# Weighted side steps, residual tiles one ahead, and inverse roots for four tiles at a time in a hybrid gMLP and state-space layer

## The chip, the cores and the metric

The kernel runs on one core of one Trainium2 chip. The metric is the device time of one execution, in microseconds (us). Engines are named as the profile names them: PE (TensorE, its weight loads as PEld), DVE (VectorE), ACT (ScalarE), POOL (GpSimd), and SP (SyncE), whose queue issues every DMA of this kernel in order.

## The reference

One layer over 2048 latent tokens of width 1024, in fp32. Cut to what matters here:

```
hl  = rms(x) * norm1_w * (1 + sc1) + sh1
proj = hl @ w_in                               # u, v (1024 each), z (1024), x/B/C (1536), dt
xbc = silu(conv5(x/B/C)); dt = softplus(dt + bias)
y   = scan_forward + scan_backward + xs * D    # 16 heads, 2 groups, state 128, chunks of 128 tokens
g   = (y * silu(z)) split in 2 groups of 512
ssd_out = rms(g over each group) * ssd_norm_w
u, v = gelu(u), gelu(v)
v   = rms(v over each head of 128) * gm_norm_w
gm_out = u * (W_s @ v + b_s)                   # 128x128 mixing per head and chunk
x   = x + g1 * (concat(gm_out, ssd_out) @ w_out)
x   = x + g2 * swiglu(rms(x) * norm2_w * (1 + sc2) + sh2)
out = rms(x) * final_norm_w
```

## The kernel before

Matrix products run as three fp32r products of high and low parts (`mm3`, lines 221 to 232): each weight tile and each activation tile is split into a rounded high part (ACT copy) and the remainder (DVE subtraction). One "product" below is a 128x512 output tile, 24 matmuls of 512 columns. The product tiles are in four PSUM banks (`mmp`), what the side work needs in four others (`smp`).

The tokens are worked in two blocks of 1024, block 1 first (projections v, u, z, then x/B/C), then block 0. After the x/B/C projection of block 0 comes the phase that the change is about. It has a main chain and a side chain, both Python generators that are interleaved when the program is written:

- Main chain: `proj_z(0)` (16 products), `proj_v(0)` (16), `proj_u(0)` (16), then three of the four parts of the output projection, `out_half(1,0)`, `out_half(0,0)` and `out_half(0,1)` (block, half; 16 products each). Half 0 takes the gMLP output, half 1 the scan output.
- Side chain: `ssd_bwd` (the backward states, 16 steps), then `ssd_y`, which goes over 16 chunks and 2 groups: `y_seg` (decay matrices: two DMAs of decay rows from `fscr`, 16 small operations on ACT and as many on DVE, an exponential, a POOL product), `y_out` (three products with py, pf and pb, sums, D term, product with z from `zscr`, sum of squares by ACT), `y_norm` (inverse root of both groups by `newton`, and two ACT copies with it as scale), `y_store` (four PE transposes per group, an ACT copy, a DMA to `sscr`).

`run` gives the main chain one step and the side chain 2.74 steps (SIDE) in turn, whatever the steps cost. The order of the generators sets the priorities of the instructions; each engine then executes its own queue in order, and the tile framework that emits the program may still move an instruction past others of its engine. `early` calls `load_mix` when the main chain has `lead` products left in a part, so that the next part's operands are loaded and split: 8 tiles for each half block, from `gmscr` or `sscr`, into `xin` buffers (8 exist) and then into `actt` buffers (16 exist, all taken by one part's operands).

`newton` (lines 234 to 244) computes an inverse root on a narrow tile by 11 small DVE operations. `proj_v` calls it once per product tile for 4 heads, `y_norm` once per chunk for 2 groups.

`out_half` computes, for each product, `t = product * g1 + t` with the residual tile t, which it loads into a buffer after the product's matmuls in program order (line 849), adds (line 850) and stores to `x2scr` (line 851). In half 1 it also sums squares, and `rstd_store` turns the sum into the inverse root for the next norm.

The last part, `out_half(1,1)`, runs beside `border()`, which prepares operands of the FFN (`prep_hl`, tiles kept for later in `cscr`). Then the buffers of the projections are given back, `hl_back` and `hl_split` (lines 978, 979, 1044) bring the FFN's operands, and `ffn1(0)` starts (matmuls at lines 1093 to 1095). In `ffn2` 16 residual tiles are held, the first NT2B in a pool of their own, the others in `t2` (14 buffers).

Of the kernel before, what the change touches and what calls it, by code (L numbers as in the profile page):

```python
# [14 lines left out]
P = 128  # L15
# [6 lines left out]
TB = 512  # L22
# [7 lines left out]
NT2B = 3  # L30
# [7 lines left out]
SIDE = 2.74  # L38
# [44 lines left out]
def kernel(ctx: ExitStack, tc: tile.TileContext, xT, ctxp, cc, crow, wad1, wad2, vecs, rows,  # L83
# [47 lines left out]
    rscr = [tc.dram_tile([1, TB], F32, name=f"rscr{i}") for i in range(4)]  # L131
    r2scr = [tc.dram_tile([1, TB], F32, name=f"r2scr{i}") for i in range(4)]
# [457 lines left out]
    def proj_u(blk, hs):  # L590
        for h0 in range(0, 8, 2):
            us = [unit(U_U + h0), unit(U_U + h0 + 1)]
            for j in range(2):
                ts_ = slice((blk * 2 + j) * TB, (blk * 2 + j + 1) * TB)
                for i, (hi, lo) in enumerate(us):
# [7 lines left out]
                    yield  # L603

    def proj_v(blk, hs):
# [17 lines left out]
        for hh in range(2):  # L623
            us = [unit(U_V + hh * 4 + i) for i in range(4)]
            for j in range(2):
                vh = []
                for c in range(4):
                    ps = mmp()
                    mm3(ps, stat_terms(hs, j * 4 + c, us, 0))
                    v = gelu2(ps, xin)  # L630
                    sq = tmp()
                    ms = sml()[:, :4]
                    for h in range(4):
                        S.activation(sq[:, h * P:(h + 1) * P], v[:, h * P:(h + 1) * P], AF.Square, accum_out=ms[:, h:h + 1])
                    V.tensor_scalar(out=ms, in0=ms, scalar1=1.0 / P, scalar2=4 * EPS, op0=ALU.mult, op1=ALU.add)
                    r = newton(ms, 4)
                    V.tensor_tensor(out=v[:, :TB].rearrange("p (a b) -> p a b", b=P), in0=v[:, :TB].rearrange("p (a b) -> p a b", b=P),
                                    in1=bc(r.rearrange("p (a o) -> p a o", o=1), P), op=ALU.mult)
                    vh.append(v)
                    if c == 1 and prev is not None:  # L640
                        mixing(*prev)
                    yield
                prev = (hh, j, vh)
        mixing(*prev)
        yield

    def proj_z(blk, hs):
        for g in range(2):
            us = [unit(U_Z + g * 4 + i) for i in range(4)]
            for c in range(8):  # L650
# [6 lines left out]
                yield  # L657
# [42 lines left out]
    def ssd_bwd(rp, hp, chunks):  # L700
        for c in chunks:
            for g in range(2):
# [4 lines left out]
                yield  # L707
# [7 lines left out]
    def y_seg(st, c, g):  # L715
        rc = st["rc"]
        Gt = []
        for q in range(2):
# [16 lines left out]
            yield  # L735
# [8 lines left out]
        yield  # L744

    def y_out(st, c, g, ms):
# [11 lines left out]
        yield  # L758
# [9 lines left out]
        yield  # L768
# [3 lines left out]
        S.activation(zt, ya, AF.Square, accum_out=ms[:, g:g + 1])  # L772
        yield
        return ya

    def y_norm(ys, ms):
        V.tensor_scalar(out=ms, in0=ms, scalar1=1.0 / TB, scalar2=4 * EPS, op0=ALU.mult, op1=ALU.add)
        r = newton(ms, 2)
        for g in range(2):
            S.activation(ys[g], ys[g], AF.Copy, scale=r[:, g:g + 1])  # L780
        yield

    def y_store(ys, c):
        for g in range(2):
            ps = smp()
            for i in range(4):
                PE.transpose(out=ps[:, i * P:(i + 1) * P], in_=ys[g][:, i * P:(i + 1) * P], identity=ident)
            t = tma()[:, :TB]
            S.copy(t, ps)
            DMA.dma_start(sscr[c // 4][g * TB:(g + 1) * TB, (c % 4) * P:(c % 4 + 1) * P].rearrange("(i p) t -> p i t", p=P),  # L790
                          t.rearrange("p (i t) -> p i t", t=P))
            yield

    def ssd_y(rp):
# [5 lines left out]
        ys, ms, norm, store = [], None, None, None  # L800
        for i, (c, g) in enumerate(its):
            if i + 1 < len(its):
                yield from y_seg(st[i + 1], *its[i + 1])
            if norm is not None:
                yield from y_norm(*norm[:2])
                norm, store = None, (norm[0], norm[2])
            if g == 0:
                ys, ms = [], sml()[:, :2]
            y = yield from y_out(st.pop(i), c, g, ms)
            ys.append(y)  # L810
            if i + 2 < len(its):
                st[i + 2] = y_load(rp, *its[i + 2])
            if store is not None and g == 0:
                yield from y_store(*store)
                store = None
            if g == 1:
                norm = (ys, ms, c)
        yield from y_norm(*norm[:2])
        yield from y_store(norm[0], norm[2])

    def load_mix(tb, half):
        hj = []
        for k in range(KT):
# [4 lines left out]
            else:  # L828
                DMA.dma_start(t[:, :TB], sscr[tb][k * P:(k + 1) * P, :])
                sn = vec[:, V_SN + k:V_SN + k + 1]  # L830
            a = actt()
# [5 lines left out]
    def out_half(blk, half, hs, tmp=tma, last=None, last_acc=None):  # L837
        acc = [None, None]
        pend = None
        for m0 in range(0, 8, 2):  # L840
            us = [unit(U_O + half * 8 + m0), unit(U_O + half * 8 + m0 + 1)]
            for j in range(2):
                ts_ = slice((blk * 2 + j) * TB, (blk * 2 + j + 1) * TB)
                for i, (hi, lo) in enumerate(us):
# [3 lines left out]
                    t = tmp()  # L848
                    DMA.dma_start(t[:, :TB], xT[m * P:(m + 1) * P, ts_] if half == 0 else x2scr[m][:, ts_])
# [5 lines left out]
                    if half == 1:  # L855
                        acc[j] = sq_acc(acc[j], t[:, :TB], last_acc if last_acc and j == 1 and m == 0 else tmp)
                        if m == 7:
                            pend = (acc[j], r2scr[blk * 2 + j], tmp)
                            if j == 1:
                                if last is None:  # L860
                                    rstd_store(*pend)
                                else:
                                    last.append(pend)
                                pend = None
                    yield

    def early(gen, total, lead, fn, box):
        for i in range(total):
            if i == total - lead:
                box.extend(fn())  # L870
            if next(gen, 0) is StopIteration:
                break
            yield
        yield from gen
# [70 lines left out]
    for _ in xbc(0, hs, None, dt_block(0, stat(hs))):  # L945
        pass
    m1, m0, s0, s1, h2 = [], [], [], [], []
    run((chain(proj_z(0, hs), proj_v(0, hs), early(proj_u(0, hs), 16, 6, lambda: [load_mix(2, 0), load_mix(3, 0)], m1),
               early(out_half(1, 0, m1), 16, 4, lambda: [load_mix(0, 0), load_mix(1, 0)], m0),
               early(out_half(0, 0, m0), 16, 4, lambda: [load_mix(0, 1), load_mix(1, 1)], s0),  # L950
               early(out_half(0, 1, s0), 16, 2, lambda: [load_mix(2, 1), load_mix(3, 1)], s1)), 1),
# [416 lines left out]
```

## Time and profile before

| | |
|---|---|
| median of 3 runs | 3001.41 us (2999.85 to 3001.45) |
| profiled execution | 3001.86 us, span 2999.7 us |
| PE busy | 2827.3 us, 94% of the span |
| DVE, ACT, POOL busy | 2002.9, 1295.7, 633.1 us (67%, 43%, 21%) |
| mean granted PE clock | 0.97 of full speed |
| DMA | 525.94 MB, 175 GB/s |

A line of a waits view reads: engine, tile and line that waited, what released it, the sum of the waits in us, their number, the longest. "L787 <- ACT tma L780" is then: line 787's instruction waited until ACT had done line 780 on tile tma. A line of a lines view gives the operation, its operands, the count, the busy time in us and the mean of one in ns, and after the second bar the engine's idle time before them with what ended it. In a timeline the first number is the start in us from the beginning of the span, the second the duration, and a bracket at the end is the idle time before with its releaser. PEclk is the granted clock of PE as a share of full speed.

### The profile page before, as it was taken

To read this page: it belongs to the slowest core of one execution; us is meant where nothing else is said; L and a number is where in the kernel's file an instruction comes from. 1 tells how busy PE (TensorE), PEld (TensorE's weight loads), DVE (VectorE), ACT (ScalarE), POOL (GpSimd) and SP (SyncE) were. 2 spreads that over 40 slices of the span, in tenths; PEclk is the share of its full clock that TensorE was granted. 3 is DMA by queue.
4 is the path that set the end of the run, shared out by engine and by line. 5 is a ranking of instruction groups with operands and counts; after the bars stand their busy time and mean duration, and the time that the engine had idled before them with its cause. 6 is when DMAs were issued, how large, how long until landed. Compare 5 with 4: busy or idle time off the path is not lost. (4 is left out here: it accounts for less than half of the span.)

```text
span 2999.7 us, 37193 instructions
## 1 busy us (share of the span) xinstructions
PE 2827.3 (94%) x12474; PEld 2253.5 (75%) x12474; DVE 2002.9 (67%) x3412; ACT 1295.7 (43%) x2387; POOL 633.1 (21%) x550
## 2 busy tenths in 40 slices
PE   7999999999998988999888799999999899999997
PEld 2788778878676767777767588888778788888885
DVE  6777966886788889778764555555776544445555
ACT  4444343344355556445452533333554333333443
POOL 3100000210131223222202244444110322221000
PEclk8999999999999999999999899999999999999998
DMA  5222567732754668877756544445766433224664
GB/s 222 88 91 88 186 217 231 261 120 82 231 168 148 194 203 254 242 244 235 210 163 221 172 158 159 160 158 165 256 224 206 142 106 106 96 100 131 226 193 157
DMA packets 295531, 525.94 MB, mean 175 GB/s; under 512 B 28838, under 2 KB 89638, under 8 KB 295340
## 3 DMA queue, kind: packets, MB, share of 16 engines
q1 hardware_dynamic: 295340, 523.57, 54.4%
q8 instruction: 98, 1.61, 0.2%
q14 instruction: 93, 0.76, 0.1%
HBM read 380.84 MB, written 142.62 MB: 175 GB/s over the span
## 5 line engine op out<-in xcount | busy, mean ns | idle before, releaser
L979 DVE TENSOR_TENSOR hl<-w,hl 128x1024 fp32r<-128x1024 f32 x286 | 371.9, 1306 | 308.9 <-ACT hl L978 127.1
L978 ACT CAST hl<-w 128x1024 fp32r<-128x1024 f32 x286 | 298.3, 1049 | 427.4 <-PE mmp L1094 121.5
L230 PE MATMUL mmp<-actt,whi 128*128 128x512 f32 x1120 | 458.2, 409 | 14.4 <-DVE t L850 8.0
L231 PE MATMUL mmp<-actt,whi 128*128 128x512 f32 x1120 | 448.5, 400 | 0.0
L232 PE MATMUL mmp<-actt,wlo 128*128 128x512 f32 x1120 | 445.8, 398 | 0.0
L1093 PE MATMUL mmp<-hl,hl 128*128 128x512 f32 x704 | 276.2, 392 | 5.5 <-DVE t L1201 2.3
L1095 PE MATMUL mmp<-hl,hl 128*128 128x512 f32 x704 | 276.0, 392 | 0.5 <-DVE hl L979 0.5
L1094 PE MATMUL mmp<-hl,hl 128*128 128x512 f32 x704 | 275.8, 392 | 0.0
L230 PEld LDWEIGHTS mmp<-actt,whi 128*128 128x128 f32 x1120 | 216.4, 193 | 65.9 <-DVE t L850 10.5
L231 PEld LDWEIGHTS mmp<-actt,whi 128*128 128x128 f32 x1120 | 216.4, 193 | 48.5 <-issue 5.5
L232 PEld LDWEIGHTS mmp<-actt,wlo 128*128 128x128 f32 x1120 | 215.6, 193 | 47.8 <-issue 1.7
L1093 PE MATMUL smp<-hl,hl 128*128 128x512 f32 x528 | 210.1, 398 | 16.5 <-ACT hl L978 16.5
L230 PE MATMUL mmp<-whi,actt 128*128 128x512 f32 x512 | 211.8, 414 | 0.0
L1094 PE MATMUL smp<-hl,hl 128*128 128x512 f32 x528 | 208.9, 396 | 0.0
L1095 PE MATMUL smp<-hl,hl 128*128 128x512 f32 x528 | 207.4, 393 | 0.0
L232 PE MATMUL mmp<-whi,actt 128*128 128x512 f32 x512 | 207.2, 405 | 0.0
L231 PE MATMUL mmp<-wlo,actt 128*128 128x512 f32 x512 | 205.8, 402 | 0.0
L985 DVE TENSOR_TENSOR t<-smp,t 128x512 f32<-128x512 f32 x88 | 60.5, 688 | 187.8 <-PE smp L1095 146.5
L1093 PEld LDWEIGHTS mmp<-hl,hl 128*128 128x128 f32 x704 | 132.4, 188 | 36.1 <-issue 2.7
L452 DVE SCALAR_TENSOR_TENSOR tma<-xin,cw,tma 128x512 f32<-128x512 f32 x192 | 144.3, 751 | 21.5 <-ACT tma L450 15.9
L985 POOL TENSOR_TENSOR w<-w 128x512 f32<-128x512 f32 x44 | 58.6, 1333 | 458.5 <-DVE hl L979 316.9
L733 POOL TENSOR_TENSOR tma<-tma 128x512 f32<-128x512 f32 x64 | 87.4, 1366 | 318.9 <-ACT tma L732 222.4
(267 smaller groups left out, 5875.7 us busy)
## 6 DMA issues: line engine op xcount, KB each, us to landing
w<-in_wall_dram SPq DMA_DIRECT2D x110, 512.0 KB, 4.1
ws<-in_wall_dram SPq DMA_DIRECT2D x104, 512.0 KB, 4.4
ascr<-t SPq DMA_DIRECT2D x154, 256.0 KB, 4.0
w<-ascr SPq DMA_DIRECT2D x154, 256.0 KB, 2.8
tma<-fscr SPq DMA_DIRECT2D x128, 256.0 KB, 5.8
w<-wscr SPq DMA_DIRECT2D x88, 256.0 KB, 3.5
t<-x2scr SPq DMA_DIRECT2D x74, 256.0 KB, 4.6
w<-in_wall_dram SPq DMA_DIRECT2D x66, 256.0 KB, 3.6
```

Source lines behind the costliest of these rows:

```text
L230: PE.matmul(ps, lhsT=lh, rhs=rh, start=(i == 0), stop=False)
L231: PE.matmul(ps, lhsT=lh, rhs=rl, start=False, stop=False)
L232: PE.matmul(ps, lhsT=ll, rhs=rh, start=False, stop=(i == n - 1))
L452: V.scalar_tensor_tensor(out=acc[:, :n], in0=raw[:, j:j + n], scalar=cw[:, ch, j:j + 1], in1=acc[:, :n], op0=ALU.mult, op1=ALU.add)
L733: G.tensor_tensor(out=A, in0=A, in1=fb, op=ALU.mult)
L978: S.copy(hi, x)
L979: eng.tensor_tensor(out=lo, in0=x, in1=hi.bitcast(F32), op=ALU.subtract)
L985: eng.tensor_tensor(out=o, in0=a, in1=b, op=ALU.add)
L1093: PE.matmul(ps, lhsT=hi[:, ms_], rhs=t[:, 0, :], start=first and k == 0, stop=False, skip_group_check=not first)
L1094: PE.matmul(ps, lhsT=hi[:, ms_], rhs=t[:, 1, :], start=False, stop=False, skip_group_check=not first)
L1095: PE.matmul(ps, lhsT=lo[:, ms_], rhs=t[:, 0, :], start=False, stop=k == 3, skip_group_check=not first)
```

## The change

- **Pacing.** `run` with SIDE is replaced for this phase by `paced`. Every step now yields a pair of weights, its estimated us on PE and on DVE; after each main step side steps are taken as long as the sum of the DVE weights is below SHARE (1.05) times the sum of the PE weights. A main step may instead yield a number of chunks that must have been stored, and side steps are taken until that is so. A side step that needs a z tile not yet written hands the turn back.
- **Scan output.** `y_norm` goes. `y_store` transposes and stores the scan output without its inverse root, one iteration of (chunk, group) later. The sums of squares of four chunks and two groups are gathered in one tile; `y_rstd` computes their inverse roots at once, transposes them on PE and stores them as two rows to `r3scr`. `load_mix` for half 1 broadcasts each row and multiplies every tile with the row and the weight on DVE, then makes the high part by an ACT copy and the low part by a DVE subtraction (before: ACT with the weight as scale, then one DVE operation).
- **v.** The sums of squares of four product tiles are gathered; `newton` runs once for 16 columns after the fourth, and the four tiles are normalised then. The mixing of the group before moves from the second to the third product. This holds for both blocks.
- **Residual tiles.** `out_half` loads the residual tile of the next product before it adds and stores the current one.
- **Rest.** The load in `early` is issued after the product at which it was issued before. In `out_half(1,1)` the two calls of `rstd_store` move behind step 1 of `ffn1(0)`; their sums lie in a pool of 2 buffers (was 1), and the pool of `ffn2`'s first residual tiles has 2 (was 3).

```diff
-SIDE = 2.74
+SHARE = 1.05
+W_MM = 5.4
+W_Z, W_V, W_U, W_O = 1.4, 2.0, 2.8, 1.45
+W_VM, W_VN, W_MIX = 3.0, 6.0, (11.4, 23.0)
+W_ST, W_SEG, W_Y1, W_Y2, W_Y3, W_NORM, W_TR = (0.85, 2.1), (0, 3.2), (2.9, 1.4), (0.85, 3.0), (0, 0.7), (0, 3.7), (1.0, 0)
...
     def proj_v(blk, hs):
...
                 vh = []
+                ms = sml()[:, :16]
                 for c in range(4):
...
-                    V.tensor_scalar(out=ms, in0=ms, scalar1=1.0 / P, scalar2=4 * EPS, op0=ALU.mult, op1=ALU.add)
-                    r = newton(ms, 4)
+                    vh.append(v)
+                    if c == 2 and prev is not None:
+                        mixing(*prev)
+                        yield W_MM, W_V + W_VM
+                    elif c < 3:
+                        yield W_MM, W_V
+                V.tensor_scalar(out=ms, in0=ms, scalar1=1.0 / P, scalar2=4 * EPS, op0=ALU.mult, op1=ALU.add)
+                r = newton(ms, 16)
+                for c, v in enumerate(vh):
                     V.tensor_tensor(out=v[:, :TB]..., in1=bc(r[:, c * 4:c * 4 + 4]..., P), op=ALU.mult)
+                yield W_MM, W_V + W_VN
...
     def y_out(st, c, g, ms):
...
+        while zdone[0] < min(g * 8 + c + 1, g * 8 + 8):
+            yield None
...
-    def y_norm(ys, ms):
+    def y_store(ya, c, g):
...
+    def y_rstd(tb, ms):
+        V.tensor_scalar(out=ms, in0=ms, scalar1=1.0 / TB, scalar2=4 * EPS, op0=ALU.mult, op1=ALU.add)
+        r = newton(ms, 8)
+        yield W_NORM
+        ps = smp()
+        PE.transpose(out=ps[0:8, :P], in_=r, identity=ident)
+        t = tma()
+        S.copy(t[0:8, :P], ps[0:8, :P])
+        DMA.dma_start(r3scr[tb].rearrange("g (c x) -> (g c) x", x=P), t[0:8, :P])
...
     def load_mix(tb, half):
+        if half == 1:
+            rb = [load_rb(r3scr[tb][g:g + 1, :], tma) for g in range(2)]
...
+                V.scalar_tensor_tensor(out=t[:, :TB], in0=t[:, :TB], scalar=sn, in1=rb[k // 4][:, :TB], op0=ALU.mult, op1=ALU.mult)
+                a = actt()
+                S.copy(a[:, 0, :], t[:, :TB])
+                V.tensor_tensor(out=a[:, 1, :], in0=t[:, :TB], in1=a[:, 0, :].bitcast(F32), op=ALU.subtract)
...
     def out_half(blk, half, hs, tmp=tma, last=None, last_acc=None):
+        def fetch(m, j):
+            t = tmp()
+            DMA.dma_start(t[:, :TB], xT[m * P:(m + 1) * P, ts_] if half == 0 else x2scr[m][:, ts_])
+            nxt.append(t)
...
-                    t = tmp()
-                    DMA.dma_start(t[:, :TB], xT[m * P:(m + 1) * P, ts_] if half == 0 else x2scr[m][:, ts_])
+                    t = nxt.pop(0)
+                    if todo:
+                        fetch(*todo.pop(0))
                     V.scalar_tensor_tensor(out=t[:, :TB], in0=ps, scalar=m_sb[:, 16 + m, 0:1], in1=t[:, :TB], op0=ALU.mult, op1=ALU.add)
                     DMA.dma_start(x2scr[m][:, ts_], t[:, :TB])
...
+    def early(gen, total, lead, fn, box, need=0):
+        for i, w in enumerate(gen):
             if i == total - lead:
+                yield need
                 box.extend(fn())
+                yield (0, W_MIX[need > 0])
+            yield w
+
+    def paced(main, side, share):
+        pe = dve = 0.0
+        for w in main:
+            if isinstance(w, int):
+                while stored[0] < w:
+                    next(side)
+                continue
+            pe, dve = pe + w[0], dve + w[1]
+            while dve < share * pe:
+                w = next(side, None)
+                if w is None:
+                    break
+                pe, dve = pe + w[0], dve + w[1]
+        for _ in side:
+            pass
...
-            if blk == 0 and t == 0:
-                rstd_store(*box.pop())
+            if box and t == 1:
+                for b in box:
+                    rstd_store(*b)
+                box.clear()
```

## Rows read from the trace of the kernel before

**Rows 1.** The page: busy time by engine; granted PE clock in 40 slices.
```profile
PE 2827.3 (94%) x12474; PEld 2253.5 (75%) x12474; DVE 2002.9 (67%) x3412; ACT 1295.7 (43%) x2387; POOL 633.1 (21%) x550
...
PEclk8999999999999999999999899999999999999998
```

**Rows 2.** Windows by stage: start:end, length, busy us per engine, PEclk, DMA share, GB/s.
```profile
300.00:418.00 118.00, 115.21 (x528) 87.86 (x528) 100.13 (x286) 43.32 (x143) 0.00 (x0) 1.00 0.61 198
778.00:1562.00 784.00, 714.77 (x3189) 557.88 (x3187) 622.64 (x1438) 411.14 (x1040) 191.97 (x156) 0.95 0.68 210
864.00:1035.00 171.00, 150.29 (x711) 119.17 (x710) 149.52 (x451) 98.46 (x315) 35.66 (x30) 0.95 0.52 161
1657.00:1710.00 53.00, 31.72 (x113) 22.20 (x114) 34.24 (x45) 32.68 (x46) 13.02 (x9) 0.81 0.55 186
```

**Rows 3.** Waits of PE from 778 to 1562 us.
```profile
PE smp L787 <- ACT tma L780: 34.5, 9, 8.4
PE smp L615 <- DVE xin L637: 6.0, 2, 4.6
PE smp L787 <- DVE tma L757: 5.5, 1, 5.5
PE mmp L230 <- DVE tma L577: 4.8, 2, 2.4
...
PE smp L615 <- DVE tma L757: 3.0, 1, 3.0
```

**Rows 4.** Waits of PE from 1562 to 1725 us.
```profile
PE smp L1093 <- ACT hl L978: 16.5, 1, 16.5
PE mmp L230 <- DVE t L850: 8.0, 6, 3.0
```

**Rows 5.** Timeline of all engines at the longest wait of L787.
```profile
1501.97 1.28 ACT L728 ACTIVATE tma<-tma,nacs 128x128 f32<-128x128 f32 x4 [3.28 <-DMA tma<-fscr]
...
1503.73 0.15 DVE L243 SCALAR_TENSOR_TENSOR sml<-sml 128x2 f32<-128x2 f32 x1
...
1506.19 1.12 PE L787 MATMUL smp<-ident,tma 128*128 128x128 f32 x4 [8.45 <-ACT tma L780]
```

**Rows 6.** Windows view of the 8 us after that wait, columns as above.
```profile
1506.00:1514.00 8.00, 7.81 (x24) 6.38 (x25) 6.00 (x9) 3.00 (x6) 2.61 (x3) 0.62 0.42 130
```

**Rows 7.** Lines view from 778 to 1562 us.
```profile
L733 POOL TENSOR_TENSOR tma<-tma 128x512 f32<-128x512 f32 x64 | 87.4, 1366 | 318.9 <-ACT tma L732 222.4 <-issue 15.0 <-DVE sml L241 14.0
...
L764 DVE TENSOR_TENSOR tma<-tma 128x512 f32<-128x512 f32 x32 | 25.6, 801 | 0.2
...
L243 DVE SCALAR_TENSOR_TENSOR sml<-sml 128x2 f32<-128x2 f32 (+1 forms) x96 | 23.8, 251 | 1.3
L833 DVE SCALAR_TENSOR_TENSOR actt<-xin,vec,actt 128x512 fp32r<-128x512 f32 x32 | 22.6, 746 | 1.7 <-ACT actt L832 1.7
...
L765 DVE TENSOR_TENSOR tma<-tma,smp 128x512 f32<-128x512 f32 x32 | 21.8, 682 | 1.1
...
L242 DVE SCALAR_TENSOR_TENSOR sml<-sml 128x2 f32<-128x2 f32 (+1 forms) x96 | 20.9, 222 | 1.3
...
L241 DVE TENSOR_TENSOR sml<-sml 128x2 f32<-128x2 f32 (+1 forms) x96 | 20.0, 212 | 1.3
...
L239 DVE TENSOR_SCALAR sml<-sml 128x2 int32<-128x2 int32 (+1 forms) x32 | 11.4, 358 | 0.4
...
L238 DVE TENSOR_SCALAR sml<-sml 128x2 int32<-128x2 int32 (+1 forms) x32 | 8.7, 270 | 0.5
```

**Rows 8.** Timeline of SP's queue at the end of out_half(1,1).
```profile
1660.83 0.32 SPq L851 DMA_DIRECT2D x2scr<-t  x1
...
1674.39 0.32 SPq L851 DMA_DIRECT2D x2scr<-t  x1
1674.77 0.42 SPq L849 DMA_DIRECT2D t<-x2scr  x1
...
1679.14 0.33 SPq L851 DMA_DIRECT2D x2scr<-t  x1
1679.52 9.87 SPq L1044 DMA_DIRECT2D t<-cscr  x16
```

More of the change, by code (lines that the diff above doesn't have):

```diff
@@ L29 @@
 NT2A = 14
-NT2B = 3
+NT2B = 2
 NW4 = 5
@@ L771, in y_out @@
         V.tensor_tensor(out=ya, in0=ya, in1=zt, op=ALU.mult)
-        S.activation(zt, ya, AF.Square, accum_out=ms[:, g:g + 1])
-        yield
-        return ya
-    def y_norm(ys, ms):
-        V.tensor_scalar(out=ms, in0=ms, scalar1=1.0 / TB, scalar2=4 * EPS, op0=ALU.mult, op1=ALU.add)
[L778 to L792, printed above, removed]
+        S.activation(zt, ya, AF.Square, accum_out=ms)
+        yield W_Y3
+        return ya
+    def y_store(ya, c, g):
+        ps = smp()
+        for i in range(4):
+            PE.transpose(out=ps[:, i * P:(i + 1) * P], in_=ya[:, i * P:(i + 1) * P], identity=ident)
+        t = tma()[:, :TB]
+        S.copy(t, ps)
+        DMA.dma_start(sscr[c // 4][g * TB:(g + 1) * TB, (c % 4) * P:(c % 4 + 1) * P].rearrange("(i p) t -> p i t", p=P),
+                      t.rearrange("p (i t) -> p i t", t=P))
+        yield W_TR
+    def y_rstd(tb, ms):
+        V.tensor_scalar(out=ms, in0=ms, scalar1=1.0 / TB, scalar2=4 * EPS, op0=ALU.mult, op1=ALU.add)
+        r = newton(ms, 8)
+        yield W_NORM
+        ps = smp()
+        PE.transpose(out=ps[0:8, :P], in_=r, identity=ident)
+        t = tma()
+        S.copy(t[0:8, :P], ps[0:8, :P])
+        DMA.dma_start(r3scr[tb].rearrange("g (c x) -> (g c) x", x=P), t[0:8, :P])
+    stored = [0]
     def ssd_y(rp):
@@ L799, in ssd_y @@
         st[1] = y_load(rp, *its[1])
-        ys, ms, norm, store = [], None, None, None
+        store = None
         for i, (c, g) in enumerate(its):
@@ L803, in ssd_y, with done @@
                 yield from y_seg(st[i + 1], *its[i + 1])
[L804 to L810, printed above, removed]
+            if g == 0 and c % 4 == 0:
+                ms = sml()[:, :8]
+            y = yield from y_out(st.pop(i), c, g, ms[:, g * 4 + c % 4:g * 4 + c % 4 + 1])
             if i + 2 < len(its):
                 st[i + 2] = y_load(rp, *its[i + 2])
-            if store is not None and g == 0:
+            if store is not None:
                 yield from y_store(*store)
[L815 to L819, printed above, removed]
+                done(store)
+            store = (y, c, g)
+            if g == 1 and c % 4 == 3:
+                yield from y_rstd(c // 4, ms)
+        yield from y_store(*store)
+        done(store)
+    def done(store):
+        if store[2] == 1:
+            stored[0] = store[1] + 1
     def load_mix(tb, half):
         hj = []
+        if half == 1:
+            rb = [load_rb(r3scr[tb][g:g + 1, :], tma) for g in range(2)]
         for k in range(KT):
@@ L947 @@
     m1, m0, s0, s1, h2 = [], [], [], [], []
[L948 to L951, printed above, removed]
-        (chain(ssd_bwd(rp, hp, range(7, -1, -1)), ssd_y(rp)), SIDE))
+    paced(chain(proj_z(0, hs), proj_v(0, hs), early(proj_u(0, hs), 16, 6, lambda: [load_mix(2, 0), load_mix(3, 0)], m1),
+                early(out_half(1, 0, m1), 16, 4, lambda: [load_mix(0, 0), load_mix(1, 0)], m0),
+                early(out_half(0, 0, m0), 16, 4, lambda: [load_mix(0, 1), load_mix(1, 1)], s0, 8),
+                early(out_half(0, 1, s0), 16, 2, lambda: [load_mix(2, 1), load_mix(3, 1)], s1, 16)),
+          chain(ssd_bwd(rp, hp, range(7, -1, -1)), ssd_y(rp)), SHARE)
     mix.close()
```

56 lines of the change are left out of this document (27 added, 29 removed).

## The prediction

> **What bounds the kernel now.** The page comes first: TensorE (PE) is busy 94% of the span and VectorE (DVE) 67% [rows 1], so time can be won only where PE stops or runs on a low clock, and the slices of PEclk in [rows 1] say where: the middle, from about 780 to 1710 us. This is the paced phase (blocks of proj_z, proj_v, proj_u and three out_half calls, with the scan beside them), then out_half(1,1), then the start of the FFN.
>
> The windows by stage come next [rows 2]. In the paced phase (778 to 1562, 784 us) PE is busy 714.8, so idle 69.2, at a mean clock of 0.95. DVE is busy 622.6 there (79%), but unevenly: 149.5 of 171 us (87%) in proj_v. From 1657 to 1710 PE works 31.7 of 53 us at 0.81.
>
> Then the waits of PE. In the paced phase one wait stands out: the transposes of y_store (L787) wait for the normalising copy of y_norm (L780), 34.5 us in 9 waits; the next are 6.0, 5.5, 4.8 and 3.0 us [rows 3]. The other 34.7 us of idle time are many small waits on DVE or on what follows DVE. After 1562 it is 16.5 us once, on a split of an FFN operand (L978), and 8.0 us in 6 waits for residual adds (L850) to free a PSUM bank [rows 4].
>
> The timeline of the longest L780 wait shows how it comes about [rows 5]: ACT waits 3.28 us for decay rows from DRAM (fscr), DVE's in-order queue stands behind that, the last Newton step (L243) starts on DVE only at 1503.7, ACT's copy behind it, and PE starts at 1506.2 after 8.45 us. So the wait is a latency chain DVE, ACT, PE, put into PE's queue. The clock pays too: granted 0.62 in the 8 us after it [rows 6], that is mostly the lower of its two levels (1.2 of 2.4 GHz), and costs 0.38 x 8 = 3.0 us, 0.36 per idle us. Over the phase 0.05 x 784 = 39 us at 69.2 idle give 0.57, an upper bound since PE also idles at the low level. I take 0.45: an idle microsecond is worth 1.45.
>
> **The change, part by part.** The sum is made against the profiled execution, 3001.86 us (span 2999.7 and 2.2 around it), 0.45 above the median of 3001.41: no difference here.
>
> *(a) y_norm goes; y_store transposes the raw scan output one iteration later.* Nothing of Newton or ACT stands before L787; what it reads was finished a whole y_out earlier. 32 ACT copies go, off the path. All L780 waits go: 34.5 x 1.45 = **-50**. What is late next: SP and ACT still wait for fscr, but PE can run on until its four mmp banks are full. If that cover is too small, up to half comes back (bound -25).
>
> *(b) y_rstd, 4 times.* Newton for 8 columns, then a transpose of r, in PE's queue with a copy and a small DMA behind. The trace has no such wait; the nearest is L780's, 34.5 us over 16 groups, 2.16 each. 4 x 2.16 x 1.45 = **+12.5**. Bounds: nothing (filled by products), or 4 x 8.4 x 1.45 = 49 (each as the longest). I take the mean, since the chain is the same without the ACT copy. Behind it wait the products on PE, and on SP, behind the store of r and at half 1 the two broadcast loads of it, the next residual load, which the tile in hand covers.
>
> *(c) Less DVE work, spread by weights.* One Newton call (L238, L239, and three rounds of L241 to L243) costs 84.8 us / 32 = 2.65 us [rows 7]. Calls in the paced phase fall from 32 to 8: 24 x 2.65 = 64 us of DVE less. load_mix of the scan half gains one operation per tile, 32 x 0.68 to 0.80 (L765, L764) = 22 to 26 us. Net about -40 of 622.6. In proj_v alone 12 calls go, 32 of 149.5 us. The weights then choose how many side steps follow a main step. By the weights in the diff, chunk and group cost the side 2.9 + 0.85 + 1.0 = 4.75 on PE and 2 x 3.2 + 1.4 + 3.0 + 0.7 = 11.5 on DVE; times 32, with ssd_bwd's 16 steps (13.6 and 33.6) and 4 Newton calls (14.8), that is 166 and 416. The main chain is 96 x 5.4 = 518, and 22 + 65 + 45 + 70 for z, v, u, out and 69 for the loads = 271. Totals 684 and 687 against a share of 1.05: at the last demand (all 16 chunks, one main step to go) 1.05 x 679 = 713 is allowed and, without the last load and step, 662 used, so the side is through by then and no step is drained unpaced; at the demand for 8 chunks 14 are ready. The DVE waits of proj_v, 6.0 + 4.8 us [rows 3], should go: 10.8 x 1.45 = 15.7, a third of the other idle time's 34.7 x 1.45 = 50. I take **-17**; bounds 0 and -50.
>
> *(d) Residual tiles one ahead, in out_half(1,1).* The load is queued on SP ahead of the store that waits for DVE, so L850 no longer waits for it: 8.0 us [rows 4], **-8**; bounds 0 and -11.6 (with the clock). In the other out_halves the same wait leaves DVE idle, not PE: nothing beyond (c). One more tma is held (14 exist); y_norm held more than that.
>
> *(e) Start of the FFN.* SP's timeline [rows 8]: the last three residual stores leave at 1660.8, 1674.4 (its L850 stands in DVE's queue behind the rstd chain of j = 0) and 1679.1, each load issued only behind the store before it, and only then 16 reads of cscr go out, whose splits PE awaits. With loads ahead and both rstd_store calls moved behind FFN step 1, the reads follow the last product directly. Of 16.5 us I leave the split of four tiles, 4 x 0.68 = 2.7: -13.8, and 2 us of the clock there (0.81): **-16**; bounds 0 and -20.
>
> *(f) proj_v of block 1* loses 12 Newton calls, 32 us of DVE's 100 in 300 to 418, but PE idles only 2.8 there [rows 2]: **-2** (0 to -3). Four unnormalised tiles and four of the last group fill the 8 xin buffers exactly; mixing moves from the second to the third product for it.
>
> *(g) The last load_mix* is issued after the last but one product, where it was before it. Per tile 0.75 + 0.68 = 1.43 us of DVE (L833, L765); 8 tiles 11.5, covered by one product of 5.4 us (W_MM): **+6**. The lower bound is 0. For the upper one, L764 (two SBUF inputs) takes 801 ns where L765 (one input from PSUM) takes 682, and the new tile operations are of L764's kind; with a whole POOL product of 1.37 us (L733) ahead of each tile it is 8 x 2.8 - 5.4 = +17 [rows 7]. I keep +6, since the side's POOL work ends ten main steps earlier.
> The Trainium skill ("SBUF — State Buffer", Who interferes with whom) speaks against this part: a DVE instruction with two SBUF inputs and a GpSimd instruction that reads SBUF exclude each other, and the later one waits for the whole of the first. The 119 ns between the two rows agree in kind. By the rule, with POOL busy throughout, the load would cost +17 and the time be 2938; by the row's mean, 8 x 0.12 = 1 us more than I take.
>
> *At nothing:* one x2 buffer fewer (t2b from 3 to 2: ffn2 then has 14 tiles of t2 in use, not 13) and a second acc buffer; the FFN's PE at full clock hides it, and a stall like (d)'s, +8, is the price if not. The two late rstd_store calls lie beside FFN products with ACT a third busy.
>
> Sum: -50 + 12.5 - 17 - 8 - 16 - 2 + 6 = -74.5, so 3001.86 - 74.5 = **2927 us**, call it 2928.
>
> **The rivals.**
> *A, the stalls move.* L780's waits are DVE backlog, and PE stops at evictions a little later: half of (a), none of (c): -25 + 12.5 - 8 - 16 - 2 + 6 = -32.5, **2969**. For it: DVE at 87% in proj_v. Against: block 1's proj_v has DVE at 85% (100.1 of 118) and PE at 98%, clock 1.00 [rows 2].
> *B, the whole phase gets as smooth as that.* (a) whole, (b) +4, (c) -40, (d) -8, (e) -18, (f) -3, (g) 0: -115, **2887**. For it: the same row. Against: the scan's chains through four engines remain.
> *C, slower: PSUM banks of the scan.* y_out takes py, pf, pb and pS, all four smp banks; its steps now come in one burst behind a product with y_store in it, and the fifth bank is there only when DVE has read pf. Such waits exist: for L757, 5.5 and 3.0 us [rows 3]. The smaller at each of 32 y_store calls: 96 us, 3001.86 - 74.5 + 96 = **3023**. It decides from 74.5/32 = 2.3 us per call. Against: two such waits in the whole phase now.
> *D, the residual loads don't move,* because SP's order is planned apart from the program's: (d) and (e) fall out, -50.5, **2951**. With A and (g) at +17 it is no change: 3001.86 - 32.5 + 24 + 11 = 3004.
>
> **How the numbers follow.** Forecast 0.45, A 0.18, B 0.17, D 0.08, C 0.08, A with D 0.04. A difference under 0.2% (6 us) can't be told from none. Faster 0.88, same 0.04, slower 0.08. The range holds the forecast, A, D and most of B: 2880 to 2985.
>
> **What would show it.** (a) L787 waits for nothing on ACT. (b) Four short waits of the r transposes. (c) Newton lines a quarter as many, and PE's clock at 0.97 or more from 778 on; the phase 60 us shorter. (d), (e) L850 without DMA waits, the cscr reads within 3 us of the last product of out_half, L1093's wait under 4 us. (g) A PE gap of some 6 us on the load's subtraction. Wrong it would be if PE's idle time in the phase stayed above 50 us, with smp or mmp banks as the releaser.

## The result and the profile after

The change makes the kernel slower: 3020.63 us (median of 4 runs, 3017.11 to 3021.9) against 3000.63 us (4 runs, 2996.12 to 3001.45); ratio 1.0068, 95% interval 1.005 to 1.0085. Forecast were 2928 us and a range that ended at 2985. The profiled execution has a span of 3020.1 us, 20.4 over that of before.

The page after, to be read beside [rows 1]: DVE is busy 17 us less and PE 3 us less, in a longer span. So it is waiting that grew, not work.

```profile
PE 2824.2 (94%) x12478; PEld 2253.9 (75%) x12478; DVE 1985.9 (66%) x3012; ACT 1277.6 (42%) x2360; POOL 638.0 (21%) x550
...
PEclk8999999999999999998999999999999999999998
```

Where it grew shows when both spans are cut at the same events. Windows of the kernel before (start:end, length, busy us per engine, PEclk, DMA share, GB/s): proj_z, then proj_v with proj_u, the three out_half calls, and all of these, the paced phase:

```profile
754.10:864.00 109.90, 105.91 (x437) 77.64 (x436) 83.00 (x163) 43.14 (x106) 23.44 (x19) 0.98 0.67 216
864.00:1176.60 312.60, 279.93 (x1285) 218.96 (x1284) 266.29 (x697) 178.04 (x500) 78.89 (x62) 0.95 0.61 192
1176.60:1561.10 384.50, 351.73 (x1553) 276.37 (x1551) 288.55 (x607) 191.48 (x437) 89.64 (x75) 0.95 0.73 224
754.10:1561.10 807.00, 737.56 (x3272) 572.96 (x3270) 637.83 (x1463) 412.66 (x1042) 191.97 (x156) 0.95 0.68 211
```

The same four of the kernel after, and the one that answers to the last of [rows 2]:

```profile
764.10:901.50 137.40, 128.60 (x533) 91.78 (x532) 110.19 (x211) 60.95 (x160) 39.69 (x31) 0.98 0.70 223
901.50:1174.00 272.50, 241.91 (x1123) 193.28 (x1122) 209.75 (x414) 146.01 (x417) 58.03 (x46) 0.95 0.59 183
1174.00:1599.80 425.80, 374.90 (x1643) 291.48 (x1642) 305.50 (x582) 185.02 (x436) 97.81 (x79) 0.94 0.71 213
764.10:1599.80 835.70, 745.42 (x3296) 576.54 (x3294) 625.43 (x1204) 391.97 (x1012) 195.54 (x156) 0.95 0.67 205
1695.00:1748.00 53.00, 48.05 (x190) 37.58 (x191) 36.20 (x43) 33.79 (x46) 21.09 (x16) 0.92 0.48 169
```

The phase is 28.7 us longer: proj_z +27.5, proj_v and proj_u -40.1, the out_halves +41.3. PE is idle 90.3 us of it (835.70 less 745.42), 69.4 before. Ahead of it block 1 lost 10.0 us (the phase starts at 764.1, not 754.1). Behind it 18 us were won: 13.4 to the first product of the FFN, 8.9 in the FFN's first half, less 4.0 in the rest.

Waits of PE in the phase, beside [rows 3]: no wait for the normalising copy is left. In its place the transposes of y_store (L793) wait 52.7 us, in 15 waits, for DVE's reads of the banks pf and pb (L768, L769).

```profile
PE smp L793 <- DVE tma L769: 28.8, 7, 8.0
PE smp L793 <- DVE tma L768: 23.9, 8, 5.7
PE smp L806 <- DVE sml L248: 9.8, 3, 4.4
PE smp L620 <- DMA gw<-in_gmw_dram: 8.8, 7, 4.0
PE mmp L235 <- DVE tma L889: 4.9, 1, 4.9
```

The timeline of the longest of them, beside [rows 5]:

```profile
1249.85 0.67 SPq L734 DMA_DIRECT2D tma<-fscr  x1
...
1251.58 0.38 SPq L735 DMA_DIRECT2D tma<-fscr  x1
...
1257.47 1.28 ACT L740 ACTIVATE tma<-tma,nacs 128x128 f32<-128x128 f32 x4 [2.87 <-DMA tma<-fscr]
...
1260.52 0.69 ACT L740 ACTIVATE tma<-tma,nacs 128x128 f32<-128x128 f32 x2 [1.77 <-DMA tma<-fscr]
1261.01 0.61 DVE L741 SCALAR_TENSOR_TENSOR tma<-tma,acs 128x128 f32<-128x128 f32 x2 [1.64 <-ACT tma L740]
...
1261.54 0.68 DVE L769 TENSOR_TENSOR tma<-smp,eac 128x512 f32<-128x512 f32 x1
...
1262.28 1.12 PE L793 MATMUL smp<-ident,tma 128*128 128x128 f32 x4 [7.99 <-DVE tma L769]
```

It has the head of the old chain. Decay rows are fetched from 1249.9 to 1251.6, ACT goes on with the first at 1257.5 and with the last at 1260.5, DVE's L741 of the next half stands behind ACT in DVE's queue, L769 behind L741, and PE's next instruction behind L769. Before, Newton's steps stood where L769 stands now.

At the FFN's start, beside [rows 4] and [rows 8], waits of PE from 1600 to 1760 us, and SP's queue:

```profile
PE mmp L235 <- DVE t L889: 4.4, 3, 2.5
PE mmp L1146 <- ACT hl L1031: 4.4, 1, 4.4
```
```profile
1684.03 0.36 SPq L890 DMA_DIRECT2D x2scr<-t  x1
1684.44 1.15 SPq L1254 DMA_DIRECT2D x2t<-x2scr  x2
1689.93 0.32 SPq L890 DMA_DIRECT2D x2scr<-t  x1
1690.29 9.21 SPq L1097 DMA_DIRECT2D t<-cscr  x16
```

The 16 reads stand directly behind the last store, and 16.5 us of waiting became 4.4.

### The profile page after: what moved, and what is told of

Its sections match the earlier page's. It is cut to its first block, busy times and chain, and to the rows that moved or that the text cites. A ratio compares the mean times of both kernels' runs of the same rounds, so it can differ in the third digit from the quotient of the medians.

```text
span 3020.1 us, 36797 instructions
## 1 busy us (share of the span) xinstructions
PE 2824.2 (94%) x12478; PEld 2253.9 (75%) x12478; DVE 1985.9 (66%) x3012; ACT 1277.6 (42%) x2360; POOL 638.0 (21%) x550
## 5 line engine op out<-in xcount | busy, mean ns | idle before, releaser
L235 PE MATMUL mmp<-whi,actt 128*128 128x512 f32 x512 | 214.2, 418 | 12.2 <-DVE tma L666 12.2
L221 ACT CAST whi<-ws 128x1024 fp32r<-128x1024 f32 x104 | 108.5, 1044 | 118.1 <-PE mmp L236 69.6
```

What stands on the lines that cost most here:

```text
L235: PE.matmul(ps, lhsT=lh, rhs=rh, start=(i == 0), stop=False)
```

## The experiments

Ratios are to the kernel before, run on the same chip; brackets hold 95% intervals, and 0.001 is 3 us. Two theories stood on record at the start: the banks (rival C of the prediction: y_store needs a fifth one), and a backlog (PE stops because DVE is held up behind ACT and the decay rows). That the weights ask more of the scan than its chain can pass came only after e2, with g2.

**e1, y_store in front of y_out**

```
+            if store is not None: yield from y_store(*store); done(store)
             y = yield from y_out(...)
-            if store is not None: yield from y_store(*store); done(store)
```

> The changed kernel with y_store of the iteration before moved from behind y_out to in front of it, nothing else. Theory 1 (banks): y_out holds py, pf, pb and pS, and y_store directly behind it needs a fifth smp bank, so PE waits until DVE has read pf or pb (28.8 + 23.9 = 52.7 us in 15 waits in the changed kernel). In front of y_out the banks of the iteration before have been read: these waits go to under 10 us in total, and with the clock (1.45 per us) the time falls by some 70 us, from 3021 to about 2950. Theory 2 (backlog): DVE stands behind ACT and the decay rows, and whatever PE does next waits for it: the waits turn up at other lines, PE's idle time in the paced phase stays within 15 us of that of the changed kernel, and the time stays between 3010 and 3025.

2997.63 us, ratio 1.0008 [0.9996, 1.002]. 18 us come back, where the one theory had 70 and the other none; PE is idle 74.5 us in the phase, 90.3 in after. So with the weights the place of y_store is worth some of the loss; with an even pace it wasn't tried. The waits of L793 for L768 and L769 go; three others take their place:

```profile
PE smp L773 <- ACT tma L795: 23.5, 7, 5.5
PE smp L793 <- DVE tma L785: 20.4, 10, 3.3
PE smp L773 <- DVE tma L769: 9.9, 9, 2.7
```

**f1, y_store's bank from the products' pool**

```
     def y_store(ya, c, g):
-        ps = smp()
+        ps = mmp()
```

> The changed kernel with the PSUM bank of y_store's transposes taken from the four product banks instead of the four of the side work; order and pacing as changed. With y_store moved in front of y_out the waits had only changed place (pS for ACT's copy of the transposes, 23.5 us; the transposes for the scan output, 20.4), 76 us in all. Theory 1 (a fifth bank is wanted in each iteration): with a bank from elsewhere the 52.7 us of the transposes for DVE's reads go, nothing stands for ACT's copy, and the time falls from 3020 to 2950 to 2985. Theory 2 (backlog of DVE and ACT behind the decay rows): the waits move to products for lack of product banks or to other lines, PE's idle time stays within 15 us, time 3005 to 3025.

3022.04 us, 1.0082 [1.0063, 1.0101]: nothing comes back. L793 no longer waits for a bank read, and the transposes of the roots (L806) wait 30.5 us instead. So a fifth bank isn't what is missing: taken from there, it only chooses who waits.

**e2, even pace** (2.6 side steps after each product; no weights)

```
-            pe, dve = pe + w[0], dve + w[1]
-            while dve < share * pe:
+            pe += share if w[0] else 0       # share 2.6
+            while pe >= 1:
```

> The changed kernel with the weights left out of the pacing: 2.6 side steps for every product, whatever they weigh (the kernel before had 2.74 of its steps). Theory 1 (banks, through the packing): with a fixed rate products of the main chain lie between y_out's steps and y_store more often, so that PE's waits of y_store for DVE's reads of pf and pb fall from 52.7 us to under 25 and the time to 2960 to 2985. Theory 2 (backlog): no change of these waits beyond 15 us, time 3010 to 3030. Theory 3: the place of y_store alone makes the wait, so the pace does nothing and e1 does all.

2982.58 us, 0.9953 [0.9939, 0.9966]: 34 us under after. The weights lose that much, with the 12 us wait of block 1 still in both. This is the outcome that the theory of the banks forecast (L793 waits 18.6 us for L768 and L769), and not the one of the backlog, which had no change; what speaks against the banks is f1.

**e4, proj_v of block 1 as before; f2, e2 with the load inside a projection in its old place**

```
# e4, proj_v, behind the squares of one product tile
+                    if blk == 1:          # roots and scaling of this tile at once
+                        r = newton(m4, 4); V.tensor_tensor(out=v..., in1=bc(r...), op=ALU.mult)
# f2, early: the projection's next product is asked for behind the load
-        for i, w in enumerate(gen):
+        while True:
             if i == total - lead: yield need; box.extend(fn()); yield (0, ...)
+            w = next(gen, None)
```

> The changed kernel with proj_v of block 1 as before (inverse roots per product tile, mixing at the second product); block 0 as changed. In the changed kernel ACT stands 12.0 us in proj_z of block 1 for a buffer that DVE's normalisation of the next block's input reads last, and PE 12.2 us behind it; the kernel before has no such wait. Theory: which buffer that tile gets follows from the order of the instructions before it, and proj_v's new order is what changed it: the wait goes, 3020.6 - 10 = about 3010. Rival: it comes from something else and stays: 3017 to 3024.

> The even pace of the run before (2.6 side steps per product), and the loads of the next part's operands issued ahead of the product again, as in the kernel before. The 10 to 12 us for which PE stands in proj_z of block 1 stayed when proj_v of block 1 was put back; the other edit there is that this load comes one product later. Theory: issued ahead of the product, its row tile takes another buffer, ACT's tanh no longer waits for DVE's last read of it, and the wait goes; the last load of scan output has two products as cover again (4.8 us of waits on its tiles now): 2982.6 - 10 - 4 = 2968. Rival: the wait comes from the pool as such: 2978 to 2987.

e4: 3013.41 us, 1.0064 [1.0051, 1.0077]. f2: 2979.49 us, 0.9940 [0.9925, 0.9955]. These are about a stop of PE in block 1 (12.2 us), of which the trace after shows ACT's side:

```profile
574.15 0.60 ACT L665 ACTIVATE tma<-mmp 128x512 f32<-128x512 f32 x1 [12.00 <-DVE xin L294]
```

PE's stop is still 10.3 us in e4 and 2.6 us in f2. So it isn't proj_v's, as e4's theory had it. In the new `early` one more product stands ahead of the load, and its tanh (L665) waits for L294, the instruction of the load that reads the inverse-root row; both tiles come from the same 14 buffers, so I take it to be a wait for the row's buffer. That the buffer makes the stop isn't shown: in f2 and h3 ACT's tanh still waits 9.9 and 10.3 us, for another reader (L193), and PE stops 2.6 and 2.9 us only. Nor did f2 gain what was expected of it (14 us): against e2 it is 0.0013, within the intervals.

**h3, after with that load in its old place** (f2's edit of `early` alone; weights kept)

> After with only the load inside a projection put back ahead of its product (one product earlier, as before). Theory (the stop of 12 us in block 1 is ScalarE waiting for the row tile's buffer, since the load is issued one product later): that wait falls under 4 us and the time by 5 to 12, to 3008 to 3015; f2, the same with an even pace, then stands for the weights alone, some 30 us under it. Rival (the load's place matters nothing with the weights, as f2 against e2 was within their intervals): 3017 to 3022.

3010.66 us, 1.0036 [1.0023, 1.005]. So with the weights the load's place cost 0.0032, 9.6 us, and the weights alone, from f2 to h3, 0.0096, 29 us. In the phase (828.5 and 802.7 us) this is idle time of PE, 89.7 us with the weights and 62.3 without, and what differs most is how long L793 waits, in h3 and then in f2:

```profile
PE smp L793 <- DVE tma L769: 27.2, 8, 7.5
PE smp L793 <- DVE tma L768: 25.4, 8, 6.6
```
```profile
PE smp L793 <- DVE tma L768: 14.1, 3, 6.4
...
PE smp L793 <- DVE tma L769: 4.6, 2, 2.8
```

**g2, a lower share**

```
-SHARE = 1.05
+SHARE = 0.985
```

> The kernel after with one constant changed: the share of side work per product 0.985 in place of 1.05, so that the side's last step comes behind product 13 of the last out_half, not behind product 3. Theory (the weights are slow because they ask the side for more steps per product than its chain of loads, ScalarE, VectorE and GpSimd can pass, in the z and out_half stages): a lower share takes back part of it, 2995 to 3008, with the z stage at 125 to 132 us. Rival (the loss lies in how the weights spread the steps over the stages, many beside z and out_half, few beside v and u, whatever the share): within 5 us of after, 3015 to 3022. Second rival (an even number of steps is no better in itself, the weights lose only by ending early): down to e2's 2980 to 2985.

3002.47 us, 1.0033 [1.002, 1.0045], proj_z 128.4 us: as the theory said, a third of what separates the weights from the even pace. Two thirds stay. What the weights do to the scan shows in DVE's first read of a bank, which runs once per scan half (chunk and group), 32 times. Of before, after, f2 and g2, in this order (times of the first and the last start):

```profile
L756 DVE TENSOR_TENSOR tma<-smp,eac x32: 673/680/684, 819.0 to 1519.4; 128x512 f32<-128x512 f32 x32
```
```profile
L768 DVE TENSOR_TENSOR tma<-smp,eac x32: 675/680/689, 823.7 to 1505.8; 128x512 f32<-128x512 f32 x32
```
```profile
L768 DVE TENSOR_TENSOR tma<-smp,eac x32: 672/682/693, 812.5 to 1510.9; 128x512 f32<-128x512 f32 x32
```
```profile
L768 DVE TENSOR_TENSOR tma<-smp,eac x32: 669/678/684, 826.3 to 1547.2; 128x512 f32<-128x512 f32 x32
```

Divided by 31, a half takes 22.6, 22.0, 22.5 and 23.3 us on average. Behind the start of the last half the phase goes on for 41.7, 94.0, 44.2 and 41.2 us. From before to after that is 52.3 us more of products with hardly any scan beside them, 18.3 less for the scan (0.59 x 31) and 5.3 less ahead of the first half: +28.7, the whole difference of the phase. This is bookkeeping and no cause, and the averages hide the pattern. Single halves of after, from DVE's timeline:

```profile
921.05 0.68 DVE L768 TENSOR_TENSOR tma<-smp,eac 128x512 f32<-128x512 f32 x1
...
936.76 0.68 DVE L768 TENSOR_TENSOR tma<-smp,eac 128x512 f32<-128x512 f32 x1
...
986.80 0.69 DVE L768 TENSOR_TENSOR tma<-smp,eac 128x512 f32<-128x512 f32 x1
```

In after 20 of the 31 steps from start to start are under 20 us (12 in f2), and six are 35 to 53 us, in proj_v and about the loads of the next operands, whose steps carry the largest DVE weights. So the weights do hurry the halves in some stretches, hold them back in others, and on average win 0.6 us a half. PE stops where the halves are packed: there L793 waits some 48 of its 52.7 us, in the six long steps some 4. With the lower share the long end is gone, but steps of 48 and 58 us stay, and so do 56.2 us of L793's waits for L768 and L769. That fits the rival on record for g2, that the loss lies in how the weights spread the steps; no run tried weights with another spread.

**e3, residual tiles only** (before, with what the change does in and behind out_half)

```
+        fetch(*todo.pop(0))                     # ahead of the loop
-                    t = tmp(); DMA.dma_start(t[:, :TB], ...)
+                    t = nxt.pop(0)
+                    if todo: fetch(*todo.pop(0))
-    accp bufs=1; NT2B = 3; rstd_store(*box.pop()) at t == 0
+    accp bufs=2; NT2B = 2; every rstd_store of box at t == 1
```

> The kernel before with only the residual tile loaded one product ahead and the two rstd_store calls of the last part moved behind FFN step 1 (accumulators in 2 buffers, first pool of x2 tiles 2). My theory: out_half(1,1) and the start of the FFN gain what the changed kernel shows there, 13 + 9 = 22 us, so 3000.6 - 22 = 2978. Rival: those gains came from the other order of the whole program and the loads alone move nothing: 2993 to 3005. Second rival: held tiles tighten the pool of 14 and the paced phase gets slower by more than it gains: above 3005.

2982.79 us, 0.9950 [0.9937, 0.9964]: 15 us won, where 22 were expected. The copy's wait stays:

```profile
PE smp L787 <- ACT tma L780: 46.4, 11, 10.8
```

**f3, f2 with decay rows a half step ahead; f5, the same with after's weights**

```
+    frow = {}
+    def f_load(n): ...           # the two DMAs of y_seg, for half step n
             n = c * 4 + g * 2 + q
             f_load(n); fb, bb = frow[n]
+            f_load(n + 1)
```

> As the run with even pace and the load ahead of the product, and the decay rows of the next half step (fscr, two tiles) loaded one half step ahead. Theory 2 (backlog): ACT's waits for these rows (88.7 us in 42 waits in the changed kernel) fall under 30 us, DVE's waits behind them too, and with them PE's waits for scan tiles and banks: 25 to 40 us less than that run, so about 2935. Theory 1 (banks): ACT's waits fall and PE's don't: within 8 us of that run. Third: two more tiles held of the pool of 14 make SP wait for buffers and it gets slower.

> The changed kernel, weights and all, with the decay rows loaded one half step ahead and nothing else. Theory 2 (backlog): the 52.7 us that y_store's transposes wait for DVE's reads fall by half or more, 3020 - 40 = 2980. Theory 1 (banks, by the packing of the steps): they fall by less than a quarter, time above 3008.

f3: 2946.0 us, 0.9819 [0.9802, 0.9837], 36 us under f2. f5: 2979.18 us, 0.9929 [0.991, 0.9947], 42 us under after, and still 33 over f3: the weights' loss stays. Both times are as expected, both waits are not: ACT's waits for the rows fall from 91.8 us in f2 to 64.6 only (under 30 was expected), DVE's behind them (L741, in f3 L753) from 58.1 to 26.7, and in f5 L793's kind (there L805) still waits 38.5 us for the bank reads, where half of 52.7 was expected.

**g1, h1, h2: the square.** g1 is e3 with the rows ahead. h1 is e3 with the scan output normalised in the load (even pace, load in its old place, proj_v as before). h2 is h1 with the rows ahead.

```
# h1, against f2: proj_v's roots per tile in both blocks, as in e4
-                    if blk == 1:
+                    if True:
```

> The kernel before with the residual tile one ahead (as in e3) and the decay rows of the next half step loaded ahead (as in f3); pace, normalisation and v as before. Theory (PE's in-order queue stalls because VectorE is held up behind ScalarE, which waits for the decay rows; what PE is seen to wait for is only what stands next in its queue): the rows' 30 to 45 us come off here too, though the normalising instruction is still there, 2982.8 -> 2940 to 2955, and PE's waits for ScalarE's normalisation fall below 25 us. Rival 1 (the waits for the normalisation are its own chain of squares, roots and scaling, which the rows don't touch): 2972 to 2983, waits still 40 or more. Rival 2 (moving the normalisation into the load is worth its 50 us once the rows are no longer late): f3, which has both, is 25 or more under this one.

> e3 (before with the residual tile one ahead) and of the rest only the scan output's normalisation in the projection's load: even pace, old place of the loads, proj_v's roots per tile as before. Theory (while the decay rows come late, PE stops for them whichever instruction stands in its queue, so taking the normalising copy out buys next to nothing): within 8 us of e3's 2983 and of f2's 2979. Rival 1 (the predicted term holds, -50 + 12.5 + 6 with a part of -17, and it was the v part that gave it back): 2945 to 2960. Rival 2 (the part costs by itself, and the v part hid it): 2990 or more.

> h1 with the decay rows one half step ahead. Theory (two chains stand beside each other in front of the same PE instructions, the late rows and the normalising copy, and either alone holds PE about as long as both): here, where both are gone, 25 or more under g1's 2969.6 by the same yardstick, so 2940 to 2950, while each alone (g1 and h1) gave 8 or less. Rival (the 32 us between g1 and f3 are proj_v's roots for four tiles): 2962 to 2972, close to g1.

| | rows late | rows ahead |
|---|---|---|
| copy in y_norm | e3 2982.79, 0.9950 [0.9937, 0.9964], phase 800.6 | g1 2969.59, 0.9925 [0.9913, 0.9938], phase 795.5 |
| in the load | h1 2979.48, 0.9927 [0.9909, 0.9944], phase 809.9 | h2 2940.03, 0.9799 [0.9779, 0.9818], phase 773.8 |

Each alone gives 7 us, hardly clear of the noise (their intervals overlap e3's), both 45 (0.0151). g1's expectation failed in its theory: the copy's waits stay with the rows ahead, so they are not the rows' doing alone. h2's held: two chains end at the same instructions of PE, and either alone holds PE about as long as both. PE's idle time in the phase says the same: 71.4 us in e3, 65.5 in g1, 64.8 in h1, 46.9 in h2. Not all of the 45 us lie in the phase, which is 26.8 us shorter in h2 than in e3; moving the normalisation into the load also shortens what stands behind the phase, by 14 us from e3 to h1, while in the phase h1 is the slower of the two by 9. Waits of PE in the phase, of g1, h1 and h2:

```profile
PE smp L799 <- ACT tma L792: 39.8, 8, 10.8
...
PE smp L799 <- DVE tma L768: 6.3, 1, 6.3
```
```profile
PE smp L806 <- DVE tma L781: 22.9, 4, 6.9
PE smp L819 <- DVE sml L248: 6.5, 3, 4.9
```
```profile
PE smp L818 <- DVE tma L794: 10.4, 5, 4.6
PE smp L831 <- DVE sml L248: 8.0, 3, 5.5
PE smp L620 <- DMA gw<-in_gmw_dram: 7.4, 6, 2.0
PE smp L818 <- DVE tma L793: 7.2, 4, 2.7
```

The middle fence is h1: the copy is gone, the bank reads hold PE for 22.9 us. In h2 the line that joins ACT to DVE, DVE's L766 behind ACT's L765, is down to 26.1 us from 60.0 in h1.

h1 to f2, and h2 to f3, are proj_v's roots for four tiles alone: +0.0013 and +0.0020, with overlapping intervals. They win nothing that could be measured.

**g3, f3 with the roots' transpose a step later; g4, g3 with rows two half steps ahead**

```
-                yield from y_rstd(c // 4, ms)
+                late_r.append((yield from y_rstd(c // 4, ms)))   # transpose, copy, store: in done()
# g4
             f_load(n + 1)
+            f_load(n + 2)
```

> f3 (even pace, early load, decay rows one half step ahead) with the transpose of the inverse roots put behind the next transposes of the scan output, a side step later than its roots. Theory: PE's 7.1 us of waits for the roots go and nothing waits in their place, since the row is needed far later: 2937 to 2941. Rival (as with the normalisation: the wait moves to the next instruction that needs VectorE): 2943 to 2948.

> g3 with the decay rows two half steps ahead in place of one (two more buffers of the 14 held). Theory (one half step is about 10 us, more than the 5.9 us that a row takes to land, so ScalarE's rest of 65 us of waits for them is not the latency of the load but when its buffer comes free): no gain over g3, within 4 us, or a loss where the two buffers are missed. Rival (latency still bounds): ScalarE's waits for rows under 30 us and 10 to 20 us under g3.

g3: 2943.53 us, 0.9827 [0.9813, 0.9841]; g4: 2946.26 us, 0.9837 [0.9824, 0.9851]. No gain in either. In g3 the 7.1 us of waits for the roots go, and the transposes' waits grow from 9.8 to 25.1 us. In g4 ACT waits 73.4 us for decay rows, 72.3 in g3: by then it isn't the rows' latency, and what it is stays open.

h2 has the lowest ratio: 2.0% under before (interval 1.8% to 2.2%), and 2.7% under after by the two ratios. f3's and g3's intervals overlap it.

## Why the prediction was wrong

The whole, as a chain of ratios: residual tiles (e3) -15 us, scan part (h1) -7, proj_v (f2) +4, weights (h3) +29, the load's place (after) +10; together +20. Forecast was -74.5. The -7 and the +4 are no larger than what the intervals leave open.

**(a), forecast -50.** The waits for the copy went, as said. The step that failed is "PE can run on until its four mmp banks are full". PE takes its queue in order, and the next scan instruction stands a product or two on; it waits for DVE, and DVE for ACT and the rows. [rows 5] shows that wait (3.28 us of ACT for fscr) at the head of the chain, and I priced its tail. Even the bound, half of it, was too narrow: (a), (b) and (g) with the part of (c) that isn't weights come to -7, and in the paced phase to +9 (800.6 to 809.9, one profile each). In another kernel the edit pays: with the rows ahead it is worth 0.0126, 38 us (g1 to h2), near the -31.5 of (a), (b) and (g) together, but only 22 of them lie in the phase, where the forecast put all of it.

**(b), +12.5, and (g), +6,** were right in kind and size: L806 waits 9.8 us where 8.6 were worked out ahead of the clock's part, and PE waits 4.8 us for the last load's tiles (L855 and L856).

**(c), -17: the other failed step,** and the dearest. The weights cost 29 us. Seeing DVE at 87% in proj_v [rows 2], I took DVE's load for what limits the phase, and spreading it evenly for a gain that costs nothing. The weights move scan steps out of proj_v and away from the loads and pack them elsewhere, and there PE, in order, stops for bank reads of a chain through DMA, ACT, DVE, PE and POOL: 52.6 us with the weights and 18.7 without (h3 and f2). I also worked out that the side would be through by the last demand and counted that as harmless: 13 of the last 16 products are evicted behind the start of the last half (5 before), with hardly any scan beside them. But g2 takes that long end away and wins back a third only. The saving of DVE work itself was well forecast: the busy times of DVE's lines in the phase, each line by itself, sum to 703.7 us before and 667.0 after, 36.7 less where I had 40 (Newton's lines 67.6 less, the load 20 more, and other instructions dearer, see the last section). It bought nothing; as busy time of the engine, in which overlapping ends count once, it is 12.4 us.

**(d) and (e), -24:** the two stages gave -13.4 and -8.9. Only part of it belongs to the residual tiles alone: in e3 they give -7.9 and -1.2, PE still waits 12.9 us at the start of the FFN, and that goes in h1. By what, wasn't tried.

**(f), -2:** block 1 takes 10 us more, by a part that I gave no price: the load in `early`, one product later, which is worth 9.6 us with the weights (h3) and with an even pace no more than the noise (e2 to f2). proj_v itself is neither better nor worse.

**The rivals.** A ("the stalls move") had (a) right and stayed 52 us low, without the weights. C gave 3023, close to what was measured, by a mechanism that is only half true: the bank waits that it names are there, 15 of them at 3.5 us, the burst of steps that it names is what the weights make, and e1 shows that the place of y_store in it counts. But f1 gives y_store another bank and wins nothing. What the prediction named as its own refutation, idle time above 50 us in the phase with smp banks as releaser, is what the trace after shows.

## What to carry to other kernels

A wait in an engine's in-order queue is worth its microseconds only if no second chain reaches the same place as late: follow the chain to its head (here a load issued where it is used) and take that away with it, or neither will pay. Read the rate of work beside a main chain as the single times between two equal instructions of it, not as their mean: here pacing by engine load packed the work in some stretches and held it back in others, the main engine stopped in the packed ones, and what was finished early left products that ran alone. A load moved by one instruction can cost a stop far from the phase that the change is about; give such a move a price of its own.

## What the runs showed of the hardware

The same DVE instruction took longer in one order of the program than in another. In the paced phase L743 (two SBUF operands, 128x128, 256 of them) took 393 ns in the kernel before (there L731) and 448 after; the sum after POOL's D term (512 columns) 769 and 945; in h2 L743's kind took 390 and L741's 469, which was 395 before. That is some 17 us more of DVE in the phase after, a quarter of what the Newton calls gave back. Those that read a PSUM bank (L768, L769, L777) stayed at 680 to 682 ns. What makes it so was not separated. The Trainium skill ("SBUF — State Buffer", Who interferes with whom) names GpSimd for a DVE instruction with two SBUF inputs. That only these vary here agrees with it; that POOL's busy time hardly differs (192.0 us in the phase before, 195.5 after) says that it would be a matter of when they meet, not of how much.

A row of decays spread over 128 partitions takes a median of 5.9 us from issue to landing, 5.2 in h2. Asking for it two half steps ahead shortens ACT's wait no further than one (73.4 and 72.3 us).

PE's granted clock in the paced phase was 0.95 both before and after, and 0.98 in h2; in the 8 us behind the longest wait of after it was 0.72, so much of that stretch ran at the lower of the two levels (1.2 of 2.4 GHz).
